# A decoder layer in split float32: the first loads in a pinned order on two DMA queues, the first casts and the first chunk in a new order

## The chip, the cores and the metric

The kernel runs on one core of a Trainium2 chip. The metric is the device time of one execution in microseconds, taken as the median over several executions. Engines are named as in the profile: PE (TensorE, matmul), PEld (its weight loads), DVE (VectorE), ACT (ScalarE), POOL (GpSimd) and SP (SyncE, which issues nearly all DMAs). A DMA is issued by an engine's instruction stream and then carried out by 16 DMA engines.

## What is computed

One decoder layer on x of 256 tokens by 1024 features, float32:

```
proj = x @ w_in                                  # 1024 -> 6 chunks of 512 columns
a = diff_attention(dq, dk, dv)                   # 4 heads, q/k pairs of 64, value 128
b = moba_attention(mq, mk, mv)                   # 8 heads of 64; at 256 tokens: causal attention
x = layer_norm(ALPHA * x + concat(a, b) @ w_o)
g, u = split(x @ w_ffn_in)                       # 2 x 2816 columns
x = layer_norm(ALPHA * x + (silu(g) * u) @ w_ffn_out)
```

Partial rotary embedding is applied to q and k.

## The kernel before

**Split products.** Every float32 operand is split into a high part, rounded to the matmul's fp32r type, and a low part, the remainder; a product is the sum of three matmuls, high·high, high·low and low·high (`mm3`, lines 141 to 144). So each weight that is loaded has to be cast by ACT (the high part) and subtracted by DVE (the low part; some pieces on POOL) before PE can use it.

**Units.** The weights are cut into units of 128 partitions x 4 rows x 512 columns, 1 MB each (line 70). Units 0 to 11 are the six chunks of w_in, two units a chunk; then w_o and the two FFN weights. `load_unit` (line 85) loads a unit in one to four DMAs on SP's queue into one of four buffers of the pool `wraw`; `split_gen` (line 98) casts on ACT (line 106) and subtracts on DVE or POOL (line 108). `ahead` (line 111 on) issues loads some units ahead, and `spread` (line 115) places the splits of the next units as hooks between the matmuls of a chunk.

**The start.** Seven matmuls on zeros (`WARM`, lines 153 and 154) run while the first data arrives. An Exp on a small tile (line 151) makes ACT load its function table. The transposed x, `xTr`, has 8 k-slices of 128 partitions x 256 tokens (128 KB each); unit 0 has four pieces `raw[0]` of 256 KB. Lines 181 to 188 issue their eight loads on SP's queue in the order w0, x0, x1, w1, x2-3, w2, w3, x4-7. Lines 189 to 194 cast and subtract them piece by piece: the cast of x0 on DVE (line 178 as `split_x` calls it), all other casts on ACT (lines 178 and 190), the subtractions on DVE (lines 179 and 192). Then `ahead` issues units 1 to 3 (line 205, three times four pieces of 256 KB), the rotary table, the causal mask, unit 4 and two small inputs.

**The chunks.** `proj_qkT` (line 384) computes the q and k chunks 0 to 3 transposed: for chunk 0 it runs over k = 0 to 7 and for each k over four column blocks j, each an `mm3` into PSUM tile j, so 96 matmuls of 256 columns. Then `rope` (line 236) takes each finished block through a shuffle, products and sums on DVE and POOL and on into high and low parts. Chunks 1 to 3, the scores, the softmax and the value chunks follow, then w_o, layer norm, the FFN (`ffn_rows`, `ffn_cols`, lines 601 and 602) and the output product (line 683), and the second layer norm with the stores at the end.

**What sets the order.** Each engine executes its own instructions strictly in the order in which they were compiled. That order is made at build time by the tile framework's scheduler, which goes by the program's order as a priority and by a simulated readiness, so instructions of one engine can pass each other. `tc.keep_in_program_order(ins)` ties an instruction behind the one traced before it on the same engine; it sets the order in the queue and adds no wait on data. From the ninth DMA on, an issue of SP waits until an earlier DMA has landed, because the framework's semaphores for these DMAs are reused.

Of the kernel before, what the change touches and what calls it, by code (L numbers as in the profile page):

```python
# [11 lines left out]
F32 = mybir.dt.float32  # L12
F32R = mybir.dt.float32r
BF16 = mybir.dt.bfloat16
AF = mybir.ActivationFunctionType
ALU = mybir.AluOpType

P = 128
S = 256
D = 1024  # L20
KT = D // P
# [3 lines left out]
HD = 64  # L25
HALF = 8
# [1 line left out]
ALPHA = 2.0 ** 0.25  # L28
LAMBDA0 = 0.8 - 0.6 * math.exp(-0.3 * 0)
EPS = 1e-5  # L30
WARM = 7


LOAD_PIECES = {1: 4, 2: 4, 3: 4, 4: 4, 5: 4, 6: 2, 7: 2}
# [22 lines left out]
def hybrid_layer_kernel(ctx, tc, xT, xr, w_in, w_o, w_f1, w_f2, cols, rows, lamb, rot, tri, out):  # L57
    nc = tc.nc
# [11 lines left out]
    units = []  # L70
# [11 lines left out]
    raw, hi, lo = {}, {}, {}  # L82
# [48 lines left out]
    def ahead(u, loads=4, splits=2):  # L131
        while state["load"] <= min(u + loads, NU - 1):
            n = state["load"]
            load_unit(n, LOAD_PIECES.get(n, 1))
            state["load"] += 1
        while state["split"] <= min(u + splits, NU - 1):
            n = state["split"]
            split_unit(n, SPLIT_PIECES.get(n, 2))
            state["split"] += 1
# [8 lines left out]
    nc.vector.memset(warm, 0.0)  # L148
    tbl = const.tile([P, 2], F32, name="tbl")
    nc.vector.memset(tbl, 0.0)  # L150
    nc.scalar.activation(tbl[:, 1:2], tbl[:, 0:1], AF.Exp)
    wps = psB.tile([P, 512], F32, tag="b", name="wps")
    for i in range(WARM):
        nc.tensor.matmul(wps, warm[:, :P], warm, start=True, stop=True)
# [5 lines left out]
    x_sb = mpool.tile([P, 2, D], F32, name="x_sb")  # L160
    axT = ctx.enter_context(ExitStack())
    xpool = axT.enter_context(tc.tile_pool(name="xpool", bufs=1))
    xTr = wraw.tile([P, KT, S], F32, tag="raw", name="xTr")
    xTh = xpool.tile([P, KT, S], F32R, name="xTh")
    xTl = xpool.tile([P, KT, S], F32R, name="xTl")
# [1 line left out]
    hi[0] = whi.tile([P, 4, 512], F32R, tag="hi", name="hi0")  # L167
    lo[0] = wlo.tile([P, 4, 512], F32R, tag="lo", name="lo0")

    def load_x(a, b):  # L170
        nc.sync.dma_start(xTr[:, a:b, :], xT[:, a:b, :])

    def load_w0(i):
        nc.sync.dma_start(raw[0][:, i, :], units[0][:, i, :])

    def split_x(a, b, copy=nc.scalar.copy):
        s = slice(a, b)
        copy(xTh[:, s, :], xTr[:, s, :])
        nc.vector.tensor_sub(xTl[:, s, :], xTr[:, s, :], xTh[:, s, :].bitcast(F32))

    load_w0(0)
    load_x(0, 1)
    load_x(1, 2)
    load_w0(1)
    load_x(2, 4)
    load_w0(2)
    load_w0(3)
    load_x(4, 8)
    for i in range(4):
        nc.scalar.copy(hi[0][:, i, :], raw[0][:, i, :])  # L190
        split_x(i, i + 1, nc.vector.tensor_copy if i == 0 else nc.scalar.copy)
        nc.vector.tensor_sub(lo[0][:, i, :], raw[0][:, i, :], hi[0][:, i, :].bitcast(F32))
    split_x(4, 6)
    split_x(6, 8)
    state["load"] = 1
    state["split"] = 1

    cs_sb = const.tile([P, 2, S], F32, name="cs_sb")
    mask = const.tile([P, S], F32, name="mask")
# [3 lines left out]
    cols_sb = const.tile([P, 1], F32, name="cols_sb")  # L203
    lam_in = const.tile([P, 4, HD], F32, name="lam_in")
    ahead(0, loads=3, splits=-1)
    for h in range(0, P, HD):
        nc.sync.dma_start(cs_sb[h : h + 2 * HALF, :, :], rot)
    nc.sync.dma_start(mask[:, P:], tri)
    ahead(0, splits=-1)
    nc.sync.dma_start(cols_sb, cols)  # L210
    nc.sync.dma_start(lam_in, bass.AP(tensor=lamb.tensor, offset=lamb.offset, ap=[[0, P], [HD, 4], [1, HD]]))
    ident = const.tile([P, P], F32, name="ident")
    make_identity(nc, ident)
    mhalf = const.tile([P, 8], F32, name="mhalf")
# [169 lines left out]
    def proj_qkT(c, side):  # L384

        pool, tag = (psB, "b") if c == 1 else (psA, "acc")
        pss = [pool.tile([P, 2, S], F32, tag=tag, name=f"pj{c}_{b}") for b in range(4 if c < 2 else 2)]
        kb = {0: 1, 1: 4}.get(c, KT)
        order = [(j, k0 + k) for k0 in range(0, KT, kb) for j in range(4) for k in range(kb)]
        fin = []  # L390
        ahead(2 * c, splits=-1)
        bg = spread([1] + [2] if c == 0 else [3, 4, 5] if c == 1 else [2 * c + 2, 2 * c + 3], 4, 28)
        for n, (j, k) in enumerate(order):
            if n == 16:
                ahead(2 * c + 1, splits=-1)
            for f in side.get(n, []) + bg.get(n, []):
                f()
            u, i = 2 * c + k // 4, k % 4
            ws = slice(j * P, (j + 1) * P)
            ps = pss[j][:, 0, :] if c < 2 else pss[j // 2][:, j % 2, :]  # L400
            mm3(ps, hi[u][:, i, ws], lo[u][:, i, ws], xTh[:, k, :], xTl[:, k, :], k == 0, k == KT - 1)
            if c == 1 and k == KT - 1:
                fin.append(rope(c, [j], ps[:, None, :]))
            if c > 1 and k == KT - 1 and j % 2:
                f = rope(c, [j - 1, j], pss[j // 2])
                if j == 1:
                    side.setdefault(n + (FIN2, FIN3)[c - 2][0], []).insert(0, f)
                else:
                    fin.append(f)
        if c == 0:  # L410
            for j in range(4):
                fin.append(rope(c, [j], pss[j][:, 0:1, :]))
        return fin
# [15 lines left out]
    fin = proj_qkT(0, {})  # L429
    nlam, gsub = lambda_prep()  # L430
    fin = proj_qkT(1, {FIN0[i]: [f] for i, f in enumerate(fin)})
    nc.sync.dma_start(x_sb, xr.rearrange("(t p) d -> p t d", p=P))
    alloc_group(0)
    sc = {FIN1[i]: [f] for i, f in enumerate(fin)}
    for j in range(4):
# [409 lines left out]
```

## Time and profile before

| | |
|---|---|
| median of 3 runs | 318.17 us (318.13 to 320.09) |
| the profiled execution | 317.75 us |
| its span, first to last instruction | 315.8 us |
| mean granted PE clock over the span | 0.991 |
| PE busy | 300.4 us, 95% of the span |
| DVE busy | 254.3 us, 81% |
| ACT busy | 177.7 us, 56% |

Times in the rows are microseconds from the span's start. Busy shares are averages over stages that have different limits, so the rows below are mostly from the first 20 us, where the change is made. "Idle before <-X" in a row of a timeline is the time for which the engine stood still just before that row and what ended it. The profiled execution is 2 us longer than its span, since launch and end lie outside the span.

### The profile page before, as it was taken

What the parts mean: (1) busy time and instruction counts of PE and PEld (TensorE: products, weight loads), DVE (VectorE), ACT (ScalarE), POOL (GpSimd) and SP (SyncE); (2) the same over time, 40 slices, a digit from 0 to 9 for tenths busy, and PEclk for the clock granted to TensorE, in tenths of its full rate; (3) what the DMA queues carried; (4) which work ended last, traced back from release to release, by engine and by line L of the source; (5) the groups of instructions that cost most, each with busy time, mean ns of one, the idle gap of its engine ahead of it and who ended that gap; (6) DMA issues with size and microseconds to landing.
All of it is one profiled execution on the core that took longest, in us unless ns stands there. A gap on an engine that the chain in (4) does not pass through costs nothing.

```text
span 315.8 us, 4704 instructions
## 1 busy us (share of the span) xinstructions
PE 300.4 (95%) x1720; PEld 255.6 (81%) x1720; DVE 254.3 (81%) x476; ACT 177.7 (56%) x347; POOL 36.3 (11%) x38
## 2 busy tenths in 40 slices
PE   8899899999999999999999999999999999999960
PEld 5799789867887788888888888888888887888850
DVE  3799999999977289949397598578679779989595
ACT  3857479398685328247377457656664565654000
POOL 1076553310030010100000000000000000000011
PEclk9999999999999999999999999999999999999996
DMA  6989943333376432558654664474362436630002
GB/s 176 391 282 352 413 151 135 133 136 137 141 251 211 195 133 66 222 247 301 230 157 146 230 221 151 162 268 162 126 246 66 175 103 227 236 127 0 0 33 100
DMA packets 13749, 57.17 MB, mean 181 GB/s; under 512 B 1664, under 2 KB 2432, under 8 KB 8864
## 3 DMA queue, kind: packets, MB, share of 16 engines
q1 hardware_dynamic: 13440, 54.79, 49.8%
q0 software_dynamic: 288, 2.10, 1.8%
q8 instruction: 13, 0.21, 0.3%
q14 instruction: 8, 0.07, 0.1%
HBM read 55.84 MB, written 1.05 MB: 180 GB/s over the span
## 4 chain that ended last, share of the span: by engine, by line
PE 74%; DVE 15%; DMA 4%; issue 3%; POOL 1%; ACT 1%; SPq 1%; DVEq 0%; ACTq 0%
PE fc L601 21%; PE foc L683 13%; PE fc L602 11%; DVE lo L108 4%; PE fo L683 4%; DMA raw<-in_w_in_dram 4%; PE wo L142 2%; PE fr L143 2%; PE fr L142 2%; PE wo L144 2%; PE wo L143 2%; PE fr L144 2%; PE pj L142 2%; PE pj L144 2%; PE pj L143 2%
## 5 line engine op out<-in xcount | busy, mean ns | idle before, releaser
L108 DVE TENSOR_TENSOR lo<-raw,hi 128x512 fp32r<-128x512 f32 (+2 forms) x108 | 105.6, 1001 | 20.9 <-ACT hi L106 20.8
L106 ACT CAST hi<-raw 128x512 fp32r<-128x512 f32 (+2 forms) x116 | 90.2, 827 | 22.5 <-PE wo L144 9.9
L601 PE MATMUL fc<-x1T,hi 128*128 128x512 f32 x288 | 100.1, 392 | 0.0
L602 PE MATMUL fc<-x1T,lo 128*128 128x256 f32 x288 | 80.5, 280 | 0.0
L601 PEld LDWEIGHTS fc<-x1T,hi 128*128 128x128 f32 x288 | 54.1, 188 | 11.9
L602 PEld LDWEIGHTS fc<-x1T,lo 128*128 128x128 f32 x288 | 54.0, 188 | 0.0
L142 PE MATMUL pj<-xTh,hi 128*128 128x256 f32 x128 | 36.7, 294 | 1.4 <-ACT hi L190 1.4
L144 PE MATMUL pj<-xTh,lo 128*128 128x256 f32 x128 | 35.7, 286 | 0.6 <-DVE lo L108 0.5
L143 PE MATMUL pj<-xTl,hi 128*128 128x256 f32 x128 | 36.1, 284 | 0.0
L604 ACT COPY v<-fc 128x256 f32<-128x256 f32 x36 | 13.3, 370 | 27.6 <-PE fc L602 27.6
L142 PEld LDWEIGHTS pj<-xTh,hi 128*128 128x128 f32 x128 | 24.3, 192 | 3.0 <-ACT hi L190 2.5
L144 PEld LDWEIGHTS pj<-xTh,lo 128*128 128x128 f32 x128 | 24.1, 191 | 1.3 <-DVE lo L108 0.7
L143 PEld LDWEIGHTS pj<-xTl,hi 128*128 128x128 f32 x128 | 24.5, 191 | 0.0
L605 DVE TENSOR_TENSOR v<-v,fc 128x256 f32<-128x256 f32 x36 | 15.0, 418 | 11.3 <-ACT v L604 11.2
L512 POOL TENSOR_TENSOR rsf<-rsf,mhalf 128x1 f32<-128x1 f32 x2 | 1.8, 922 | 178.6 <-DVE rsf L511 178.6
L683 PE MATMUL foc<-hi,hTl 128*128 128x512 f32 x56 | 22.1, 395 | 0.0
L683 PE MATMUL foc<-lo,hTh 128*128 128x512 f32 x56 | 22.1, 394 | 0.0
L683 PE MATMUL foc<-hi,hTh 128*128 128x512 f32 x56 | 22.1, 394 | 0.0
L108 POOL TENSOR_TENSOR lo<-raw,hi 128x512 fp32r<-128x512 f32 x8 | 13.8, 1723 | 20.1 <-ACT hi L106 20.1
L284 ACT ACTIVATE E<-E,negm 128x128 f32<-128x128 f32 (+1 forms) x32 | 14.2, 444 | 2.5 <-DVE negm L281 2.4
L247 POOL TENSOR_TENSOR sh<-sh,cs_sb 128x256 f32<-128x256 f32 (+1 forms) x12 | 13.3, 1120 | 18.2 <-DVE sh L245 17.5
L142 PE MATMUL pj<-hi,xTh 128*128 128x512 f32 x32 | 13.7, 429 | 0.0
(201 smaller groups left out, 547.5 us busy)
## 6 DMA issues: line engine op xcount, KB each, us to landing
raw<-in_w_f_dram SPq DMA_DIRECT2D x28, 1024.0 KB, 5.1
raw<-in_w_in_dram SPq DMA_DIRECT2D x24, 256.0 KB, 5.5
raw<-in_w_in_dram SPq DMA_DIRECT2D x4, 1024.0 KB, 6.3
raw<-in_w_o_dram SPq DMA_DIRECT2D x4, 1024.0 KB, 4.8
raw<-in_w_f_dram SPq DMA_DIRECT2D x10, 256.0 KB, 3.5
raw<-in_w_f_dram SPq DMA_DIRECT2D x5, 512.0 KB, 4.6
raw<-in_w_in_dram SPq DMA_DIRECT2D x4, 512.0 KB, 8.4
rows<-in_rows_dram POOLq DMA_DIRECT2D x2, 1024.0 KB, 6.6
```

Of the source, the lines that this page charges most:

```text
L106: nc.scalar.copy(h[:, s, :], r[:, s, :])
L108: eng.tensor_sub(l[:, s, :], r[:, s, :], h[:, s, :].bitcast(F32))
L142: nc.tensor.matmul(ps, sh, mh, start=first, stop=False)
L143: nc.tensor.matmul(ps, sh, ml, start=False, stop=False)
L144: nc.tensor.matmul(ps, sl, mh, start=False, stop=last)
L247: nc.gpsimd.tensor_mul(sh, sh, sin2[:, :m, :])
L284: nc.scalar.activation(e, e, AF.Exp, bias=negm[g][:, i, u : u + 1], scale=-1.0, accum_out=ls[g][:, i, u : u + 1])
L601: nc.tensor.matmul(ps, hi[u][:, i, ws], x1T[:, k], start=k == 0, stop=False)
L602: nc.tensor.matmul(ps[:, 0, :], lo[u][:, i, ws], x1T[:, k, 0, :], start=False, stop=k == KT - 1)
L604: nc.scalar.copy(v, ps[:, 1, :])
L605: nc.vector.tensor_add(v, v, ps[:, 0, :])
L683: nc.tensor.matmul(bank[name] if ps is None else ps, x, w[:, cs], start=key not in opened, stop=last and (m, i) == (len(todo) - 1, 2))
```

## The change

The Exp that loads ACT's table is traced behind the first x loads. x0, x1 and x2-3 are loaded on ACT's queue; w0 to w3 and then x4-7 on SP's queue, each pinned behind the load before it. The casts and subtractions of unit 0 and x are pinned in one order on ACT (w0, w1, x2-3, w2, w3, x4-5, x6-7) and one on DVE (x0 cast and both its parts, w0, x1 cast and parts, w1, x2-3, w2, w3, x4-5, x6-7): the cast of x1 moves from ACT to DVE, and x2 and x3 are cast together. Chunk 0 runs over k and, inside k, over the three products, each for all four blocks j: first high·high four times, then high weight by low x, then low weight by high x. Two more matmuls on zeros stand at the start. Five later loads (rotary table, mask, two small inputs, x itself) are pinned in the program's order.

```
-WARM = 7
+WARM = 9
...
-    nc.scalar.activation(tbl[:, 1:2], tbl[:, 0:1], AF.Exp)
...
-    load_w0(0)
-    load_x(0, 1)
-    load_x(1, 2)
-    load_w0(1)
-    load_x(2, 4)
-    load_w0(2)
-    load_w0(3)
-    load_x(4, 8)
-    for i in range(4):
-        nc.scalar.copy(hi[0][:, i, :], raw[0][:, i, :])
-        split_x(i, i + 1, nc.vector.tensor_copy if i == 0 else nc.scalar.copy)
-        nc.vector.tensor_sub(lo[0][:, i, :], raw[0][:, i, :], hi[0][:, i, :].bitcast(F32))
-    split_x(4, 6)
-    split_x(6, 8)
+    pin = tc.keep_in_program_order
+    nc.scalar.dma_start(xTr[:, 0:1, :], xT[:, 0:1, :])
+    for a, b in ((1, 2), (2, 4)):
+        pin(nc.scalar.dma_start(xTr[:, a:b, :], xT[:, a:b, :]))
+    pin(nc.scalar.activation(tbl[:, 1:2], tbl[:, 0:1], AF.Exp))
+    nc.sync.dma_start(raw[0][:, 0, :], units[0][:, 0, :])
+    for i in range(1, 4):
+        pin(nc.sync.dma_start(raw[0][:, i, :], units[0][:, i, :]))
+    pin(nc.sync.dma_start(xTr[:, 4:8, :], xT[:, 4:8, :]))
+    def first_hi(i):
+            h, l, src = hi[0][:, i, :], lo[0][:, i, :], raw[0][:, i, :]
+            pin(nc.scalar.copy(h, src))
+            return lambda: pin(nc.vector.tensor_sub(l, src, h.bitcast(F32)))
+    def first_x(a, b, eng=nc.scalar):
+        s = slice(a, b)
+        pin((eng.copy if eng is nc.scalar else eng.tensor_copy)(xTh[:, s, :], xTr[:, s, :]))
+        pin(nc.vector.tensor_sub(xTl[:, s, :], xTr[:, s, :], xTh[:, s, :].bitcast(F32)))
+    f = first_hi(0)
+    first_x(0, 1, nc.vector)
+    f()
+    first_x(1, 2, nc.vector)
+    first_hi(1)()
+    first_x(2, 4)
+    for i in (2, 3):
+        first_hi(i)()
+    first_x(4, 6)
+    first_x(6, 8)
...
+        for k in range(KT if c == 0 else 0):
+            u, i = k // 4, k % 4
+            for p, (w, x) in enumerate(((hi, xTh), (hi, xTl), (lo, xTh))):
+                if 4 * k + p == 16:
+                    ahead(1, splits=-1)
+                for f in bg.get(4 * k + p, []) + (bg.get(4 * k + 3, []) if p == 2 else []):
+                    f()
+                for j in range(4):
+                    nc.tensor.matmul(pss[j][:, 0, :], w[u][:, i, j * P : (j + 1) * P], x[:, k, :],
+                                     start=(k, p) == (0, 0), stop=(k, p) == (KT - 1, 2))
-        for n, (j, k) in enumerate(order):
+        for n, (j, k) in enumerate(order if c else ()):
```

## Rows read from the trace of the kernel before

**Rows 1.** Page, part 1: busy time of each engine over the span.
```profile
PE 300.4 (95%) x1720; PEld 255.6 (81%) x1720; DVE 254.3 (81%) x476; ACT 177.7 (56%) x347; POOL 36.3 (11%) x38
```

**Rows 2.** Chain of work that ended last, in order of time: start, length, what.
```profile
3.52 6.25 DMA raw<-in_w_in_dram
...
16.50 1.27 DVE lo L108
...
57.51 0.33 PE ppd L290
```

**Rows 3.** Busy time by stretch: engines with instruction counts, PEclk, DMA share, GB/s.
```profile
1.50:4.50 3.00, 2.96 (x8) 0.89 (x6) 0.54 (x2) 1.34 (x3) 0.42 (x3) 1.00 0.85 208
...
6.00:8.00 2.00, 2.00 (x17) 2.00 (x17) 0.69 (x1) 0.39 (x1) 0.00 (x0) 1.00 0.73 128
8.00:16.00 8.00, 6.63 (x54) 6.36 (x53) 6.36 (x11) 6.67 (x13) 0.13 (x1) 1.00 1.04 393
...
16.00:57.50 41.50, 39.64 (x323) 37.38 (x321) 40.96 (x114) 28.96 (x83) 24.24 (x18) 1.00 0.72 255
```

**Rows 4.** Timeline of SP, its DMA issues: start, length, line, what, count.
```profile
0.74 0.37 SPq L174 DMA_DIRECT2D raw<-in_w_in_dram  x1
1.17 0.89 SPq L171 DMA_DIRECT2D xTr<-in_xT_dram  x2
...
4.00 0.43 SPq L171 DMA_DIRECT2D xTr<-in_xT_dram  x1
4.47 9.66 SPq L95 DMA_DIRECT2D raw<-in_w_in_dram  x12
...
25.57 0.38 SPq L432 DMA_DIRECT2D x_sb<-in_xr_dram  x1
```

**Rows 5.** Timeline of ACT: start, length, line, what [idle before <-releaser].
```profile
0.74 1.28 ACT L151 ACT_TABLE_LOAD   x1 [0.74 <-PEq L835]
...
3.61 0.62 ACT L190 CAST hi<-raw 128x512 fp32r<-128x512 f32 x1 [1.38 <-DMA raw<-in_w_in_dram]
5.10 0.40 ACT L178 CAST xTh<-xTr 128x256 fp32r<-128x256 f32 x1 [0.87 <-DMA xTr<-in_xT_dram]
5.77 0.62 ACT L190 CAST hi<-raw 128x512 fp32r<-128x512 f32 x1 [0.27 <-DMA raw<-in_w_in_dram]
8.15 0.71 ACT L178 CAST xTh<-xTr 128x256 fp32r<-128x256 f32 x2 [1.76 <-DMA xTr<-in_xT_dram]
9.14 1.28 ACT L190 CAST hi<-raw 128x512 fp32r<-128x512 f32 x2 [0.27 <-DMA raw<-in_w_in_dram]
11.11 1.14 ACT L178 CAST xTh<-xTr 128x512 fp32r<-128x512 f32 x2 [0.69 <-DMA xTr<-in_xT_dram]
```

**Rows 6.** Timeline of PE: start, length, line, what, count [idle before <-releaser].
```profile
1.19 3.17 PE L154 MATMUL wps<-warm 128*128 128x512 bf16 x7 [1.19 <-DVE tbl L150]
4.40 1.20 PE L142 MATMUL pj<-xTh,hi 128*128 128x256 f32 x4
...
5.93 0.41 PE L143 MATMUL pj<-xTl,hi 128*128 128x256 f32 x1
6.15 0.41 PE L144 MATMUL pj<-xTh,lo 128*128 128x256 f32 x1
...
8.04 0.28 PE L143 MATMUL pj<-xTl,hi 128*128 128x256 f32 x1
8.16 0.28 PE L144 MATMUL pj<-xTh,lo 128*128 128x256 f32 x1
9.81 0.39 PE L142 MATMUL pj<-xTh,hi 128*128 128x256 f32 x1 [1.37 <-ACT hi L190]
```

**Rows 7.** Timeline of DVE: start, length, line, what [idle before <-releaser].
```profile
3.96 0.29 DVE L178 CAST xTh<-xTr 128x256 fp32r<-128x256 f32 x1 [2.81 <-DMA xTr<-in_xT_dram]
...
16.50 1.27 DVE L108 TENSOR_TENSOR lo<-raw,hi 128x512 fp32r<-128x512 f32 x1 [0.43 <-ACT hi L106]
...
17.77 0.45 DVE L245 STREAM_SHUFFLE sh<-pj 128x256 f32<-128x256 f32 x1
```

More of the change, by code (lines that the diff above doesn't have):

```diff
@@ L168, in hybrid_layer_kernel @@
     lo[0] = wlo.tile([P, 4, 512], F32R, tag="lo", name="lo0")
[L170 to L176, printed above, removed]
-        s = slice(a, b)
-        copy(xTh[:, s, :], xTr[:, s, :])
-        nc.vector.tensor_sub(xTl[:, s, :], xTr[:, s, :], xTh[:, s, :].bitcast(F32))
-    load_w0(0)
-    load_x(0, 1)
-    load_x(1, 2)
-    load_w0(1)
-    load_x(2, 4)
-    load_w0(2)
-    load_w0(3)
-    load_x(4, 8)
-    for i in range(4):
-        nc.scalar.copy(hi[0][:, i, :], raw[0][:, i, :])
-        split_x(i, i + 1, nc.vector.tensor_copy if i == 0 else nc.scalar.copy)
-        nc.vector.tensor_sub(lo[0][:, i, :], raw[0][:, i, :], hi[0][:, i, :].bitcast(F32))
-    split_x(4, 6)
-    split_x(6, 8)
+    pin = tc.keep_in_program_order
[12 more added lines that the diff above has]
+    def first_x(a, b, eng=nc.scalar):
+        s = slice(a, b)
+        pin((eng.copy if eng is nc.scalar else eng.tensor_copy)(xTh[:, s, :], xTr[:, s, :]))
[10 more added lines that the diff above has]
+    first_x(6, 8)
     state["load"] = 1
@@ L206, in hybrid_layer_kernel @@
     for h in range(0, P, HD):
-        nc.sync.dma_start(cs_sb[h : h + 2 * HALF, :, :], rot)
-    nc.sync.dma_start(mask[:, P:], tri)
+        pin(nc.sync.dma_start(cs_sb[h : h + 2 * HALF, :, :], rot))
+    pin(nc.sync.dma_start(mask[:, P:], tri))
     ahead(0, splits=-1)
-    nc.sync.dma_start(cols_sb, cols)
-    nc.sync.dma_start(lam_in, bass.AP(tensor=lamb.tensor, offset=lamb.offset, ap=[[0, P], [HD, 4], [1, HD]]))
+    pin(nc.sync.dma_start(cols_sb, cols))
+    pin(nc.sync.dma_start(lam_in, bass.AP(tensor=lamb.tensor, offset=lamb.offset, ap=[[0, P], [HD, 4], [1, HD]])))
     ident = const.tile([P, P], F32, name="ident")
@@ L431, in hybrid_layer_kernel @@
     fin = proj_qkT(1, {FIN0[i]: [f] for i, f in enumerate(fin)})
-    nc.sync.dma_start(x_sb, xr.rearrange("(t p) d -> p t d", p=P))
+    tc.keep_in_program_order(nc.sync.dma_start(x_sb, xr.rearrange("(t p) d -> p t d", p=P)))
     alloc_group(0)
```

## Prediction

> **What bounds the kernel now.** I read the busy times first, then the chain that ended last, then the first 20 us engine by engine. PE is busy for 300.4 of 315.8 us [rows 1], so it looks like the only limit; the chain corrects that. In order of time it goes through the DMAs of w_in from 3.52 us on, then from 16.50 through DVE's subtractions, and only from 57.51 us through PE [rows 2]. The busy table says the same: between 16 and 57.5 us DVE works 40.96 of 41.50 us, while PE, with 39.64, has 1.86 us of idle time [rows 3]. So a microsecond that PE gains at the start reaches the end only if DVE's work between 16 and 57.5 us is earlier too; and that work starts when weights have landed. From 8 to 16 us the DMA engines run at a share of 1.04 and 393 GB/s, which is all they give in this trace; before, they do worse: 208 GB/s from 1.5 to 4.5 us at a share of 0.85, and 128 GB/s from 6 to 8 us at a share of 0.73 [rows 3].
>
> The start in detail. SP issues the eight first loads one after another from 0.74 to 4.43 us and then the twelve pieces of units 1 to 3 from 4.47 on [rows 4]. Where a cast was released by a DMA, its start marks a landing: w0 by 3.61, x1 by 5.10, w1 by 5.77, x2-3 by 8.15, w2 by 9.14, x4-7 by 11.11 [rows 5]; x0 by 3.96 [rows 7]. PE does k = 0 and 1 from 4.40 to 8.44, idles 1.37 us for the high part of w2, and from 9.81 on runs without a gap worth naming through chunk 0 [rows 6].
>
> **The change part by part.** The sum is made against the profiled execution, 317.75 us, which lies 0.42 under the median of the three runs, 318.17; I add the 0.42 at the end. One per cent is 3.2 us, about what a measurement of this kernel can tell from no change, as its three runs lie up to 2 us apart.
>
> *Loads on two queues.* Three of SP's eight issues go to ACT: two of 0.89 together and one of about 0.43, so 1.3 us [rows 4]. SP's first piece of unit 1 could be issued at 3.1 instead of 4.47. The bytes and their sizes stay the same. Bounds: 0, if the DMA engines were never short of work, and 1.3 us, if the issue was all that held them. The nearest row is the share between 1.5 and 4.5 us, 0.85 [rows 3]: 15% of 3 us, 0.45, was not filled. I take 0.5 us: all landings behind the first four come 0.5 earlier, and with them the chain through unit 1 and DVE.
>
> The trace shows this as a bound by the DMA engines and not by SP, with shares of 0.85 and 1.04 [rows 3]. The Trainium skill says the same and more strongly, in "DMA: Bandwidth & Descriptors", section "Issuing engines are not separate DMA queues": loads started by different engines end on the same 16 DMA engines, and only the starting engine's issue time is saved. By that rule this part would be worth nearer to nothing than 1.3 us; it is the first rival below.
>
> *What ACT pays.* No DMA issue of ACT stands in the trace. By SP's rows one costs 0.37 to 0.45 us [rows 4], three cost 1.1 to 1.35. They push the table load of 1.28 us, which now starts at 0.74 [rows 5], to end at 3.1 to 3.4, and the small Exp behind it to 3.3 to 3.6; the first cast waits for w0 until 3.61 anyway [rows 5]. So 0. The cover behind it: PE is on its zero matmuls until 5.27 (next item), so the cast of 0.62 us may start as late as 4.6; beyond that each microsecond costs PE one, up to the idle 1.37.
>
> *Two more zero matmuls.* The seven run from 1.19 for 3.17 us, 0.45 each with the last one's tail shared out [rows 6], so nine end at 1.19 + 9 x 0.45 = 5.27. The first real matmul goes from 4.40 to 5.27, 0.87 later. The idle 1.37 us before 9.81 absorbs it [rows 6]: 0, with 0.5 of cover left, which is just what is used if w2 lands 0.5 earlier. In that stretch PE runs at the lower of its two levels, 1.2 GHz: 256 columns at 5.93 and 6.15 follow each other by 0.22 us, where at 8.04 and 8.16 it is 0.12 (2.4 GHz), although the table of stretches prints a granted clock of 1.00 throughout [rows 3, 6]. PE had been at work nearly without a pause from 1.19 when the spacing fell. Nine keep it at work without the pause before 4.40, so the rise should come no later. From below I bound this at 0 as well, since w2 and not PE sets 9.81.
>
> *Casts in a pinned order.* ACT loses x1's cast, 0.40 us, and DVE gains it at 0.29 [rows 5, 7]. x2 and x3 go as one cast and one subtraction instead of two. DVE has 2.81 us of idle time before its first cast [rows 7] and works 0.69 of the 2 us from 6 to 8 [rows 3]; ACT idles 1.76 before 8.15 [rows 5]. So 0. Without that cover it would be 0.29.
>
> *Product by product.* The same 96 matmuls at 0.12 us. The compiled order before already mixed the products: four high by high at 4.40, then singles of L143 and L144 [rows 6]. 0, between minus and plus 0.4, one or two more restarts of 0.2 us like the one at 9.81, whose neighbours start 0.22 and not 0.12 apart.
>
> *Later loads pinned.* In the trace SP issues x itself at 25.57, behind the tables and unit 4 [rows 4], which is the order of the program already. 0.
>
> *Downstream.* DVE's last idle time of note, 0.43 us at 16.50, waits for a cast of a landed piece, and the first shuffle of chunk 0 follows at 17.77 [rows 7]. With landings and chunk 0 both up to 0.5 earlier I take this wait as filled: 0.4. The bounds are 0 and 0.54, all that DVE idles between 16 and 57.5 [rows 3].
>
> Sum: 0.5 + 0.4 = 0.9 us. 317.75 - 0.9 = 316.85, and with 0.42 added, 317.3 us.
>
> **The rivals.**
>
> *Nothing moves (318.2).* The DMA engines, not the issue, set the landings of units 1 to 3, and DVE's stretch begins when it did. For it: the share of 1.04 at 393 GB/s from 8 to 16 us, and a share of 0.73 with 128 GB/s from 6 to 8, when eight DMAs had already been issued [rows 3, 4], so lack of issues was not the cause. Against: the share of 0.85 before 4.5.
>
> *The slow stretch goes (315.9).* From 6 to 8 us the engines moved 128 and not 393 GB/s; 265 x 2 us is 530 KB, 1.35 us at 393 GB/s [rows 3]. If it came from the single queue, the change removes it: 0.9 + 1.35 = 2.25 us. For it: the engines were not full. Against: there was work in the queue. If the 208 GB/s before 4.5 rose as well, 185 x 3 us or 555 KB, another 1.4 us, would give 314.5, the far end.
>
> *The weights come later (319.2, the slower side).* x's 512 KB on its own queue shares the DMA engines with w0 and w1 from the start. If each queue gets half, w1 is complete when 1024 KB have moved and no longer when 768 KB have; that is the place of x2-3 now, 8.15 instead of 5.77 [rows 5]. Its cast takes 0.62, and k = 1 needs 12 x 0.12 = 1.4 us: done at 10.2, 0.4 behind the 9.81 of today. PE would then idle from about 7 to 8.8, and if it runs at its lower level afterwards, 24 matmuls cost 0.1 more each, 2.4 us. So 0.4 to 2.8; DVE's wait at 16.50 hides 0.43 of it. I take 1.0. The point from which it decides: w1 later than 9.81 - 1.4 - 0.6 = 7.8 us. Against: k = 2 waits for w2 in any case, so a late w1 costs nothing until then.
>
> That the two queues take turns is what the Trainium skill states ("DMA: Bandwidth & Descriptors", section "Queues, rings and completion order": each DMA engine goes round the queues that have work, packet by packet); no run here shows it yet.
>
> **How the numbers follow.** The forecast 0.42, nothing moves 0.27, the slow stretch goes 0.16, the weights come later 0.15. The range from 315.2 to 319.0 holds the first two whole, most of the third and the milder part of the fourth. Faster by over 1% means under 315.0: the far end of the third, 0.06. Slower by over 1% means over 321.3, only the fourth with its lower level kept for long: 0.03. Within 1%: 0.91.
>
> **What would show it.** Right: on SP the first piece of unit 1 issued near 3.1 to 4.0; w2's cast before 9.0; the cast of x4-5 begun near 10.6 instead of 11.11; PE reaching its first transposes of the probabilities, the step at 57.51, about 0.9 earlier. Wrong: that step at 57.5 or later although PE's gap before k = 2 is gone (then DVE or the DMA engines held it); w1's cast after 7.8 (the slower rival); a DMA rate near 390 GB/s from 5 us on (the third). Wrong in size: a different compiled order of DVE's work after 16 us, which I could not read from the trace before.

## The result and the profile after

The changed kernel took 321.39 us in the median of nine runs (320.57 to 322.81), the kernel before 318.17 beside it (317.39 to 320.37): a ratio of 1.0096, with an interval of 1.0074 to 1.0118. So it is slower by about one per cent, where 317.3 us was forecast. The profiled execution took 320.62 us with a span of 318.5, against 317.75 and 315.8: 2.87 us more.

PE's busy time is the same within 0.2 us, so the loss is waiting. Page part 1 of the changed kernel, which answers to [rows 1]:

```profile
PE 300.2 (94%) x1722; PEld 255.7 (80%) x1722; DVE 254.5 (80%) x476; ACT 177.4 (56%) x345; POOL 35.2 (11%) x38
```

The start first. Timeline of SP in the changed kernel (columns as in [rows 4]):

```profile
0.74 0.38 SPq L175 DMA_DIRECT2D raw<-in_w_in_dram  x1
1.18 1.37 SPq L177 DMA_DIRECT2D raw<-in_w_in_dram  x3
2.59 0.52 SPq L178 DMA_DIRECT2D xTr<-in_xT_dram  x1
4.16 10.52 SPq L95 DMA_DIRECT2D raw<-in_w_in_dram  x12
```

And of ACT ([rows 5]):

```profile
0.74 0.40 ACTq L171 DMA_DIRECT2D xTr<-in_xT_dram  x1
1.17 0.94 ACTq L173 DMA_DIRECT2D xTr<-in_xT_dram  x2
2.14 1.28 ACT L174 ACT_TABLE_LOAD   x1 [2.14 <-issue]
3.44 0.20 ACT L174 ACTIVATE tbl<-tbl 128x1 f32<-128x1 f32 x1
3.98 0.62 ACT L182 CAST hi<-raw 128x512 fp32r<-128x512 f32 x1 [0.35 <-DMA raw<-in_w_in_dram]
5.06 0.62 ACT L182 CAST hi<-raw 128x512 fp32r<-128x512 f32 x1 [0.46 <-DMA raw<-in_w_in_dram]
9.81 0.62 ACT L187 CAST xTh<-xTr 128x512 fp32r<-128x512 f32 x1 [4.13 <-DMA xTr<-in_xT_dram]
10.33 1.14 ACT L182 CAST hi<-raw 128x512 fp32r<-128x512 f32 x2
11.70 1.14 ACT L187 CAST xTh<-xTr 128x512 fp32r<-128x512 f32 x2 [0.23 <-DMA xTr<-in_xT_dram]
```

Three things are to be seen. SP is through with the first loads at 3.11, yet the first piece of unit 1 goes out at 4.16 and not at 3.1. It is the ninth DMA and waits for x0, the first load of ACT's queue, as the chain of the changed kernel shows (start, length, what; x0 lands at 4.14, the first piece of unit 1 at 12.34):

```profile
0.74 3.40 DMA xTr<-in_xT_dram
...
4.16 8.18 DMA raw<-in_w_in_dram
```

w1 is cast at 5.06, earlier than 5.77. And x2-3, issued behind x1 on ACT's queue, is cast at 9.81 instead of 8.15; ACT works in the pinned order, so w2 and w3 stand behind it and are cast from 10.33 on instead of 9.14.

The trace records the landing of each load. w0 and x0 land at 3.96 and 4.14, w1 and x1 at 5.04 and 5.22, w2 and x2-3 at 9.62 and 9.78: the loads of the two queues arrive in pairs, one of each, although w0 and w1 carry twice the bytes of x0 and x1. The kernel before had x2-3 at 8.13 and w2 at 9.11. So x2-3 lost its lead: it was 0.98 ahead of w2 and is now 0.17 behind. In all five profiles with x2-3 on ACT's queue it is 0.17 to 0.20 behind. As its cast stands ahead of w2's, w2 is cast 0.71 after it has landed, where before it was 0.03.

w2 itself landed 0.51 later as well, and for this the bytes have to be counted. Here are the DMA queues from 6 to 8 us (queue, packets, MB, share of the 16 engines; q1 carries SP's loads, q10 ACT's):

```profile
q1 hardware_dynamic: 149, 0.34, 58.2%
q10 hardware_dynamic: 58, 0.10, 39.1%
```

ACT's queue moved less than a quarter of the bytes, for it had only x2-3 left to carry, and eight of the sixteen shares into which a load is cut had landed by 7.40; SP's queue went on with later loads. The table of stretches ([rows 3]) says how much was moved in all:

```profile
1.50:4.50 3.00, 3.00 (x8) 1.06 (x7) 0.30 (x2) 2.00 (x3) 0.42 (x3) 1.00 0.80 256
4.50:6.00 1.50, 1.50 (x7) 1.28 (x6) 1.47 (x4) 0.72 (x2) 0.00 (x0) 1.00 0.72 202
6.00:8.00 2.00, 2.00 (x15) 2.00 (x14) 0.79 (x2) 0.00 (x0) 0.00 (x0) 1.00 0.97 218
8.00:16.00 8.00, 5.98 (x51) 5.77 (x50) 5.54 (x10) 5.89 (x11) 0.00 (x0) 1.00 0.99 357
```

The second of these stretches in the kernel before:

```profile
4.50:6.00 1.50, 1.50 (x7) 1.46 (x8) 1.21 (x3) 0.63 (x2) 0.00 (x0) 1.00 0.99 357
```

More came through than before in the first and the third stretch (256 against 208 GB/s, 218 against 128), less in the second and the fourth (202 against 357, 357 against 393). Up to 8 us that makes 1.51 MB against 1.42, up to 16 us 4.36 against 4.56. The 0.2 MB that are missing take 0.5 us at 393 GB/s, and by about as much w2 and the loads behind it are late. That is no more than two executions of one kernel differ by: w2 landed at 9.95 in a second profile of the kernel before (below). PE pays first at k = 2 ([rows 6]):

```profile
1.19 4.02 PE L153 MATMUL wps<-warm 128*128 128x512 bf16 x9 [1.19 <-DVE tbl L150]
4.66 1.42 PE L407 MATMUL pj<-xTh,hi 128*128 128x256 f32 x4
...
11.00 0.75 PE L407 MATMUL pj<-xTh,hi 128*128 128x256 f32 x4 [2.02 <-ACT hi L182]
```

That is 1.19 us later than 9.81, but it isn't the end of the story: the first score matmul comes only 0.75 later (38.78 against 38.03), and then the loss grows, to 1.88 at the first transpose of the probabilities (59.00 against 57.12) and to 2.4 at the score matmuls of the next chunk (72.28 against 69.88). From about 84 us on it stays at 2.65. The first transposes before and after:

```profile
57.12 0.33 PE L289 MATMUL ppd<-ident,E 128*128 128x128 f32 x1 [0.62 <-DVE E L306]
```

```profile
59.00 0.33 PE L294 MATMUL ppd<-ident,E 128*128 128x128 f32 x1 [1.78 <-DVE E L311]
```

So some three quarters of a microsecond come from the start and two from between 43 and 74 us, where the change edits nothing. PE's waits in the changed kernel (what waited, for whom, us in total, times, longest):

```profile
PE pj L407 <- ACT hi L182: 2.0, 1, 2.0
PE ppd L294 <- DVE E L311: 1.8, 1, 1.8
PE wps L153 <- DVE tbl L150: 1.2, 1, 1.2
PE s L142 <- DVE negm L286: 1.1, 1, 1.1
```

In the kernel before, the wait of ppd is 0.6 us, and the one for negm is not in the list. Both are waits for DVE, so here is DVE's timeline between 49 and 59 us. Before:

```profile
49.60 0.74 DVE L245 STREAM_SHUFFLE sh<-pj 128x512 f32<-128x512 f32 x1
50.24 0.67 DVE L246 TENSOR_TENSOR a<-pj,cs_sb 128x512 f32<-128x512 f32 x1
50.83 1.49 DVE L108 TENSOR_TENSOR lo<-raw,hi 128x512 fp32r<-128x512 f32 x1
52.25 0.68 DVE L251 TENSOR_TENSOR a<-a,sh 128x512 f32<-128x512 f32 x1
52.85 0.24 DVE L301 RECIPROCAL rl<-ls 128x16 f32<-128x16 f32 x1
...
55.70 3.74 DVE L306 SCALAR_TENSOR_TENSOR E<-E,sc 128x128 f32<-128x128 f32 x8
```

After:

```profile
49.49 0.69 DVE L108 TENSOR_TENSOR lo<-raw,hi 128x512 fp32r<-128x512 f32 x1 [0.17 <-ACT hi L106]
...
51.22 0.74 DVE L250 STREAM_SHUFFLE sh<-pj 128x512 f32<-128x512 f32 x1
51.85 0.68 DVE L251 TENSOR_TENSOR a<-pj,cs_sb 128x512 f32<-128x512 f32 x1
52.63 0.25 DVE L306 RECIPROCAL rl<-ls 128x16 f32<-128x16 f32 x1
53.43 1.76 DVE L256 TENSOR_TENSOR a<-a,sh 128x512 f32<-128x512 f32 x1 [0.55 <-POOL sh L252]
55.11 1.28 DVE L108 TENSOR_TENSOR lo<-raw,hi 128x512 fp32r<-128x512 f32 x2
...
56.73 0.68 DVE L108 TENSOR_TENSOR lo<-raw,hi 128x512 fp32r<-128x512 f32 x1
57.33 1.23 DVE L308 TENSOR_SCALAR sc<-sc,nlam 128x8 f32<-128x8 f32 x1
58.60 2.72 DVE L311 SCALAR_TENSOR_TENSOR E<-E,sc 128x128 f32<-128x128 f32 x8
```

The same instructions stand in another order. Before, the weight split at 50.83 runs while POOL makes its part of sh, and the add behind it finds sh ready. After, that split has been taken forward to 49.49, where it waits 0.17 us for its cast, pushes the shuffle back by its own 0.6 and leaves the add to wait 0.55 for POOL. One more split (56.73) stands ahead of the scaling of E, where before it came behind. E begins 2.90 us later than before, though the score matmuls ahead of it began only 0.75 late.

The lengths of these rows say something too. The same split takes 0.68 us at 54.02 and 1.49 at 50.83, the first scaling of E 0.34 in the changed kernel and 1.36 before, the add at 53.43 takes 1.76 instead of 0.68. Each of the long ones stands beside an instruction of POOL. POOL's timeline of the kernel before:

```profile
50.49 1.28 POOL L247 TENSOR_TENSOR sh<-sh,cs_sb 128x512 f32<-128x512 f32 x1 [6.41 <-DVE sh L245]
...
55.39 1.52 POOL L108 TENSOR_TENSOR lo<-raw,hi 128x512 fp32r<-128x512 f32 x1 [1.31 <-ACT hi L106]
```

The split at 50.83 ends at 52.32, 0.55 behind POOL's 51.77, and the first scaling of E at 57.06, behind POOL's 56.91; the add at 53.43 ends at 55.19, and POOL is at work on a split of its own from 53.36 to 54.64. So these instructions of DVE got little done while POOL worked. It is not so for all: the mask products from 42.84 to 44.02 kept their usual 0.28 and 0.42 us beside POOL's work from 42.80 to 44.08. By such rows some 6 of the 40.96 us for which DVE is busy from 16 to 57.5 us are waiting beside POOL (an estimate: what an instruction lasted beyond the length it has when POOL is idle). The long first scaling is also why PE's loss at 59.00 is 1.88 and not the 2.90 of E's start. No run tried POOL's part by itself.

The order on each engine is set when the program is compiled; in the changed kernel's compiled list DVE's instructions stand otherwise in eleven places behind 43 us, and ACT's in five. The experiments separate the loads from that order.

### The profile page after: what moved, and what is told of

Same layout as the page of the kernel before. It is cut to its first block, busy times and chain, and to the rows that moved or that the text cites. A ratio compares the mean times of both kernels' runs of the same rounds, so it can differ in the third digit from the quotient of the medians.

```text
span 318.5 us, 4704 instructions
## 1 busy us (share of the span) xinstructions
PE 300.2 (94%) x1722; PEld 255.7 (80%) x1722; DVE 254.5 (80%) x476; ACT 177.4 (56%) x345; POOL 35.2 (11%) x38
## 4 chain that ended last, share of the span: by engine, by line
PE 72%; DVE 14%; DMA 5%; issue 3%; ACT 2%; POOL 2%; DVEq 0%; ACTq 0%; POOLq 0%; SPq 0%
PE fc L617 21%; PE foc L699 13%; PE fc L618 11%; DMA raw<-in_w_in_dram 4%; PE fo L699 4%; DVE lo L108 3%; PE wo L142 2%; PE fr L143 2%; PE fr L142 2%; PE wo L143 2%; PE wo L144 2%; PE fr L144 2%; PE pj L142 2%; DVE a L256 2%; PE pj L144 2%
## 5 line engine op out<-in xcount | busy, mean ns | idle before, releaser
L142 PE MATMUL pj<-xTh,hi 128*128 128x256 f32 x96 | 27.8, 289 | 0.0
L144 PE MATMUL pj<-xTh,lo 128*128 128x256 f32 x96 | 27.1, 282 | 0.4 <-DVE lo L108 0.4
L143 PE MATMUL pj<-xTl,hi 128*128 128x256 f32 x96 | 27.0, 281 | 0.0
L144 PEld LDWEIGHTS pj<-xTh,lo 128*128 128x128 f32 x96 | 18.1, 188 | 0.6 <-DVE lo L108 0.6
L142 PEld LDWEIGHTS pj<-xTh,hi 128*128 128x128 f32 x96 | 18.1, 188 | 0.5
L143 PEld LDWEIGHTS pj<-xTl,hi 128*128 128x128 f32 x96 | 18.1, 188 | 0.0
L108 POOL TENSOR_TENSOR lo<-raw,hi 128x512 fp32r<-128x512 f32 x8 | 12.8, 1606 | 20.7 <-ACT hi L106 20.7
```

What stands on the lines that cost most here:

```text
L108: eng.tensor_sub(l[:, s, :], r[:, s, :], h[:, s, :].bitcast(F32))
L142: nc.tensor.matmul(ps, sh, mh, start=first, stop=False)
L143: nc.tensor.matmul(ps, sh, ml, start=False, stop=False)
L144: nc.tensor.matmul(ps, sl, mh, start=False, stop=last)
```

## The experiments

An order can be tied without changing a wait: a table gives the instruction numbers of each engine, and each is made to follow the one before it on its own engine. The edit, common to all runs that tie an order (called ORDER below; PE's order is the same in all of them but for added zero matmuls):

```diff
+ORDER = {
+    "DVE": [
...
+    have = {i.name: i for i in nc.cur_bb.bb.instructions}
+    for chain in ORDER.values():
+        chain = [n for n in chain if f"I-{n}" in have]
+        for a, b in zip(chain, chain[1:]):
+            tc.add_manual_dep(have[f"I-{b}"], f"I-{a}",
...
```

All diffs are against the changed kernel; where a line is a list of numbers, the minus line is that kernel's compiled order and the plus line the order that the run ties, in the numbers of the changed kernel. The kernel before, run beside the experiments, had medians of 318.06, 318.18 and 318.04 us in three sets of 25, 31 and 35 runs.

**One queue, the rest kept.** The eight loads go back to SP in their old order.

```diff
-    nc.scalar.dma_start(xTr[:, 0:1, :], xT[:, 0:1, :])
-    for a, b in ((1, 2), (2, 4)):
-        pin(nc.scalar.dma_start(xTr[:, a:b, :], xT[:, a:b, :]))
...
+    pin(nc.sync.dma_start(xTr[:, 0:1, :], xT[:, 0:1, :]))
+    pin(nc.sync.dma_start(xTr[:, 1:2, :], xT[:, 1:2, :]))
+    pin(nc.sync.dma_start(raw[0][:, 1, :], units[0][:, 1, :]))
+    pin(nc.sync.dma_start(xTr[:, 2:4, :], xT[:, 2:4, :]))
...
```

> The changed kernel with its eight first loads back on SP's queue in the old order (w0, x0, x1, w1, x2-3, w2, w3, x4-7), all else as changed: nine zero matmuls, pinned casts, chunk 0 product by product. In the compiled program the orders of DVE, ACT and POOL behind unit 0 are then those of the kernel before. Theory A (x2-3 lands late on the second queue, 9.81 us instead of 8.15, and all behind it): x2-3's cast again near 8.2, PE resumes near 9.8, time about 318.2. Theory B (the compiled order of DVE, ACT and POOL after 16 us costs): also about 318.2, since that order is undone as well. Theory C (pinned casts or nine zero matmuls cost): stays near 320.5 to 321.4.

Measured: 318.38 us, ratio 1.0017 (0.9986 to 1.0048). Behind the first unit this kernel's DVE, ACT and POOL have the order of the kernel before, but for one split and one shuffle that change places near 18 us. So the zero matmuls, the pinned casts, the product order and the later pins cost nothing that can be measured; the loss hangs on the two queues and on what follows from them.

**Two queues in the old order.** The changed kernel tied to the order of the run above.

```diff
-349, 312, 315, 323, 326,
+312, 315, 323, 326, 349,
...
-756, 727, 729, 731, 733, 746, 747,
+727, 729, 731, 733, 746, 747, 756,
...
```

These are the first changed stretch of DVE's list and the first of its late part, by instruction number: 756 is the split seen at 49.49, 746 and 747 are the shuffle and the product behind it.

> The changed kernel with its loads on two queues, but every instruction of PE, DVE, ACT and POOL tied behind its predecessor in the compiled order of the one-queue kernel (which, behind unit 0, is the order of the kernel before on DVE, ACT and POOL). Theory A (late landings alone): the loss stays whole, about 321. Theory B (compiled order alone): about 318.2. Both: PE resumes at k = 2 near 11.0 and chunk 0 ends near 19.6, but the wait at the first transposes of the probabilities shrinks from 1.8 us; time between, about 319.5 to 320.

Measured: 320.78 us, 1.0056 (1.0025 to 1.0088), in two groups of times: 318.8 to 319.9 in four of ten executions, 320.8 to 321.6 in six. x2-3 is cast at 10.19 and PE idles 2.6 us ahead of k = 2; the wait of ppd is back at 0.6. The median is that of the theory that the late landing is all (about 321), but the profile isn't: with the first group the two queues by themselves cost some 0.5 us against the run above, and the second group had to be explained.

**One queue in the new order.** The converse: loads as in the first run, tied to the changed kernel's order.

```diff
-        pin(nc.scalar.dma_start(xTr[:, a:b, :], xT[:, a:b, :]))
+    pin(nc.sync.dma_start(xTr[:, 2:4, :], xT[:, 2:4, :]))
...
+ORDER = {
...
```

> The opposite mix: loads on one queue in the old order, every instruction of PE, DVE, ACT and POOL tied into the compiled order of the changed kernel. Theory A: about 318.2. Theory B: about 321, with the wait of 1.8 us at the first transposes still there. Both: about 319.5 to 320.

Measured: 320.35 us, 1.0057 (1.0033 to 1.0081), with the waits of the changed kernel: 1.8 us for E and 1.0 for negm. The order costs some 2 us with no load moved. The theory that the late landing is all (318.2) misses.

**The kernel before, once more.** No edit; a single execution.

> The kernel before, unchanged, for a second profile of its start: if the slow stretches of the DMA engines (128 GB/s from 6 to 8 us in the first profile) come by chance, they lie elsewhere here and x2-3's and w2's casts move by more than 0.5 us from 8.15 and 9.14; if they belong to the order of the loads, the casts start within 0.3 us of those.

Measured: 318.57 us. The casts of x2-3, w2 and x4-5 came 0.8 us later than in [rows 5] (8.93, 9.97, 11.95), the rate from 6 to 8 us was again low (100 GB/s), and the end was 0.82 later. Neither alternative holds: the casts moved by more than 0.5 us, but the slow stretch of the DMA engines stood in the same place. Its length differed between these two executions by about as much as the forecast meant to gain, and by as much as the changed kernel's first score matmul was late: it came at 38.88 here, against 38.03 and 38.78.

**Only the late part of the new order.** One queue; DVE from its 61st instruction and ACT from its 36th in the changed kernel's order, all ahead of that in the old one. The loads are edited as above; of the order:

```diff
-349, 312, 315, 323, 326,
+312, 315, 323, 326, 349,
...
```

> Loads on one queue; PE, POOL and the first 60 DVE instructions in the order of the kernel before, but DVE from its 61st and ACT from its 36th instruction on (the scores of the first head group and later) in the compiled order of the changed kernel. There, one subtraction of unit 8 stands before the last scores and no longer behind the second shuffle of chunk 2, where it ran while POOL multiplied. If that late part is the price of the order: about 320.2 as with the whole new order on one queue, with a wait near 1.8 us at the first transposes of the probabilities. If the early part (splits of units 3 to 5 against the rotary sums) is the price: about 318.4, with a wait near 0.6.

Measured: 320.75 us, 1.008 (1.0049 to 1.0112), again with 1.8 us for E and 1.1 for negm. The late part is the price of the order.

**Only x0 and x1 on ACT's queue**, the rest of x on SP behind w1, in the old order:

```diff
-    for a, b in ((1, 2), (2, 4)):
-        pin(nc.scalar.dma_start(xTr[:, a:b, :], xT[:, a:b, :]))
+    pin(nc.scalar.dma_start(xTr[:, 1:2, :], xT[:, 1:2, :]))
...
+    pin(nc.sync.dma_start(xTr[:, 2:4, :], xT[:, 2:4, :]))
```

> Only x0 and x1 (256 KB) on ACT's queue; x2-3 back on SP's queue behind w1; compiled order of the kernel before everywhere behind the loads. If the price of the two queues is x2-3's place on a queue of its own beside SP's long one: x2-3's cast starts by 8.9 and the time is 318.2 to 318.6, or up to 0.9 less since SP issues two loads fewer. If any second queue at the start slows the landings: w2's cast behind 10, time 319.5 or more.

Measured: 318.28 us, 0.9987 (0.9957 to 1.0017). x2-3 is cast at 7.13, a microsecond earlier than in [rows 5], but w2 still at 9.18, and PE idles 1.4 us ahead of k = 2. Both are as the first alternative had it: the price was x2-3's place. Taking two issues off SP is worth nothing that can be measured.

**x2-3 late, on one queue**: w2 and w3 are issued ahead of it, old order.

```diff
+    pin(nc.sync.dma_start(raw[0][:, 2, :], units[0][:, 2, :]))
+    pin(nc.sync.dma_start(raw[0][:, 3, :], units[0][:, 3, :]))
+    pin(nc.sync.dma_start(xTr[:, 2:4, :], xT[:, 2:4, :]))
```

> One queue, compiled order of the kernel before, but w2 and w3 are issued before x2-3. The slow stretch of the DMA engines (100 to 210 GB/s from 6 to 8 us in every one-queue profile): if it belongs to the time after the start, it stands there again; if it belongs to x2-3's transfer, it moves behind 7. ACT casts x2-3 before w2, so PE resumes when x2-3 has landed, as late as w3 did (about 10); time 318.5 to 319.5, which also says what 0.5 us of later start for k = 2 costs when the loads behind are not later.

Measured: 320.05 us, 1.0048 (1.002 to 1.0076), in two groups again: 318.4 to 319.4 in five executions, 320.7 to 321.8 in five. The median misses the 318.5 to 319.5 expected; the first group is about there. The slow stretch stands again from 6 to 8 us, with 180 GB/s. The profiled execution is of the second group. Its table of stretches:

```profile
8.00:10.00 2.00, 0.39 (x4) 0.18 (x2) 0.00 (x0) 0.61 (x2) 0.00 (x0) 1.00 1.03 339
10.00:12.00 2.00, 1.42 (x7) 1.42 (x8) 1.96 (x4) 2.00 (x6) 0.00 (x0) 0.72 0.98 350
12.00:14.00 2.00, 2.00 (x12) 2.00 (x11) 2.00 (x4) 1.97 (x5) 0.00 (x0) 0.50 1.06 406
```

The seventh number is the granted clock. PE works 0.39 of the 2 us before 10; then the clock is at half, the lower level of 1.2 GHz, from about 11 us to the end of these rows. PE's timeline of the same run shows the pause of 2.19 us ahead of it and groups of four matmuls that start 0.80 apart and, next, 0.85: 0.21 for one, where 0.12 is usual here:

```profile
10.58 1.00 PE L555 MATMUL pj<-xTh,hi 128*128 128x256 f32 x4 [2.19 <-ACT hi L330]
11.38 1.05 PE L555 MATMUL pj<-xTl,hi 128*128 128x256 f32 x4
```

**Two queues, late part old.** The changed kernel with its own order up to 43 us and the old one behind (the complement of the run with the late part alone):

```diff
-756, 727, 729, 731, 733, 746, 747,
+727, 729, 731, 733, 746, 747, 756,
...
```

> The changed kernel on two queues with its own early order, but DVE from its 61st and ACT from its 36th instruction on in the order of the kernel before. If the late part of the order is worth about 1.8 us: 319.5 to 320, with the wait at the first transposes back near 0.6; if only the early part counts, 321.

Measured: 318.50 us, 1.0000 (0.9976 to 1.0023), although x2-3 is cast at 9.42 and PE idles 2.5 us ahead of k = 2. That is less than the 319.5 to 320 expected. With the late order undone and the early one kept, the change costs nothing that can be measured. It doesn't follow that two queues are free: in the wholly old order they cost some 0.5 us, above, and what the early part of the new order gives back was not tried apart.

**One late stretch of two.** DVE's 89th to 111th instruction, and ACT's casts beside them, put back:

```diff
-756, 727, 729, 731, 733, 746, 747, 804, 771, 785, 796, 773, 805, 824, 806,
+727, 729, 731, 733, 746, 747, 756, 771, 804, 805, 785, 773, 806, 796, 807,
```

Here 824 is the split at 56.73, 771 the add, 804 the reciprocal, and 807 and those behind it the scaling of E.

> The changed kernel with one stretch of its compiled order put back: VectorE's 89th to 111th instruction (mask products, the split lo8, the reciprocal, the first sums) and ScalarE's two casts beside them stand as in the kernel before; the later stretch (sums against splits behind the probabilities) stays the changed kernel's. Theory (this stretch is the larger part of the loss): the wait ahead of the first ppd matmul falls from 1.8 to 0.6 to 0.8 us, the negm wait further on stays near 1 us, and the median comes to 320.0 to 320.5 (ratio 1.005 to 1.007) against 321.4 of the changed kernel. Rival 1 (the whole loss is here): 318.3 to 319.2. Rival 2 (it is the later stretch): the ppd wait may fall but the median stays at 321 or more.

Measured: 319.81 us, 1.0064 (1.0037 to 1.009). PE's waits:

```profile
PE s L289 <- DVE negm L433: 1.4, 1, 1.4
...
PE ppd L441 <- DVE E L458: 0.6, 1, 0.6
```

The wait for E is mended, the one for negm is longer by 0.3. The ratio lies in the range of the theory, the median a little under its 320.0 to 320.5; both rivals miss. That this stretch is the larger part of the loss is not borne out: the table at the end of this section has the changed kernel lose 1.91 us behind the first score matmul, and this one 1.37.

**Zero matmuls in PE's idle stretch**, on two queues in the old order:

```diff
+                for _ in range(8 if (k, p) == (2, 0) else 0):
+                    nc.tensor.matmul(wps, warm[:, :P], warm, start=True, stop=True)
                 for j in range(4):
```

> Two queues in the old compiled order (as in e2_two_queues_old_order), plus eight zero matmuls on TensorE between the products of the second weight tile and those of the third, where it sat idle 2.6 us. Eight at 0.22 us fill about 1.8 us of that. Theory (the upper group of times, 320.8 to 321.5 in 6 of 10 executions, is a granted clock that falls after the idle stretch): the clock stays at its upper level from 8 to 16 us, the upper group is gone, and the median comes to 318.8 to 319.2. Rival (the upper group has another cause, the loads or the order): six of ten executions still read 320.8 or more and the median stays above 320.

Measured: 319.01 us (318.09 to 319.46 in twelve executions), 1.0019 (1.0000 to 1.0037). The upper group of the same kernel without them, six of ten at 320.8 or more, is gone, as the theory of the clock had it.

**The same eight on one queue** in the old order: the loads of the first run, and the lines just shown.

```diff
-        pin(nc.scalar.dma_start(xTr[:, a:b, :], xT[:, a:b, :]))
+    pin(nc.sync.dma_start(xTr[:, 2:4, :], xT[:, 2:4, :]))
...
+                for _ in range(8 if (k, p) == (2, 0) else 0):
...
```

> One queue in the old order (as in e1_one_queue, which is the kernel before but for the pins, the zero matmuls and the product order), plus the same eight zero matmuls in the idle stretch ahead of the third weight tile, 1.2 us in that profile. Theory (clock): no execution at 320 or more where e1 had three of ten; the fillers overrun the idle stretch by up to 0.6 us, so the median stands at 318.2 to 318.8. Rival: two to four of ten executions still read 320 or more; or the overrun costs more, median 319 or above.

Measured: 318.37 us (318.11 to 318.80), 1.0009 (0.9993 to 1.0024). Table of stretches:

```profile
8.00:10.00 2.00, 2.00 (x13) 1.13 (x12) 0.89 (x3) 1.24 (x2) 0.00 (x0) 1.00 0.97 340
10.00:12.00 2.00, 2.00 (x18) 1.97 (x18) 1.40 (x4) 1.37 (x3) 0.00 (x0) 1.00 1.04 380
```

PE never stops, its clock stays at the upper level, and no execution is above 319, where the first run had three of ten at 320.3 to 320.9. The median stays: what the upper times lost is saved, the others pay nothing. The run before differs from this one by the queues alone, so with PE kept at work the two queues cost 0.64 us in the old order (319.01 against 318.37).

**The best parts together**: x0 and x1 alone on ACT's queue, the changed kernel's order up to 43 us, the old one behind, and the eight zero matmuls.

```diff
+    pin(nc.sync.dma_start(xTr[:, 2:4, :], xT[:, 2:4, :]))
...
-756, 727, 729, 731, 733, 746, 747,
+727, 729, 731, 733, 746, 747, 756,
...
+                for _ in range(8 if (k, p) == (2, 0) else 0):
...
```

> The parts that measured well put together: first two tiles of x on ScalarE's queue and the rest on SyncE's (as in e6_x01_on_act), the changed kernel's compiled order up to 43 us and the old one behind it (as in e8_two_queues_late_old), and eight zero matmuls in the idle stretch. Theory: it beats both kernels slightly, 317.2 to 317.9 (ratio 0.996 to 0.999), with no execution above 319. Rival (the gains don't add, or the fillers delay the third tile's products): 318.2 to 318.8, no difference from the kernel before.

Measured: 318.07 us (317.44 to 318.89), 0.9996 (0.998 to 1.0012). It doesn't beat the kernel before in the median: it lies between the 317.2 to 317.9 of the theory and the 318.2 to 318.8 of the rival, and no difference from the kernel before is what the rival said. That no execution is above 319 is what the theory said. What it removes is the upper times: the kernel before had seven of 35 between 319.6 and 320.1 in the same set, all with a mean granted clock of 0.984 or 0.985, and this one has none of twelve.

**What the profiles of all runs say of the late part.** In each profile the time from the first score matmul to the end of the span was taken (us; the start of the first score matmul in the second column):

| | first score matmul | from there to the end |
|---|---|---|
| kernel before | 38.03 | 277.80 |
| kernel before, once more | 38.88 | 277.78 |
| one queue, the rest kept | 38.42 | 277.81 |
| two queues in the old order | 39.63 | 277.81 |
| two queues, late part old | 39.13 | 277.86 |
| changed kernel | 38.78 | 279.71 |
| one queue in the new order | 38.52 | 279.69 |
| one late stretch of two put back | 37.92 | 279.17 |

All ten profiles with the late part in the old order have 277.78 to 277.86, whatever the queues and the start; the new one adds 1.9 us. (The run with the late part alone has 281.12; its profiled execution, 323.94 us, was its slowest, and the granted clock fell in it once more, near 77 us.) Of the 1.9, 1.13 are lost up to the first transposes, by the order around 50 us, and 0.78 behind them; with the stretch around 50 us put back, 1.37 are lost behind them, so the two do not simply add.

## Why the prediction was wrong

*Right.* ACT's three issues cost what was said (1.34 us against 1.1 to 1.35), the table load and the small Exp ended at 3.42 and 3.64, a little beyond what was said, and the first cast waited for w0 all the same. The two zero matmuls, the casts, the product order and the later pins were put at nothing; all four together measured 1.0017 (0.9986 to 1.0048). One reason was wrong beside a right term: the spacing of PE's matmuls fell from 0.21 to 0.12 us at 7.15 and not at 6.4 as before, so the two more zero matmuls did not keep the rise from coming later; the pause ahead of k = 2 covered it. That SP's issue was not what held the loads was the rival "nothing moves", and the run with x0 and x1 alone on ACT's queue bears it out.

*The step "Loads on two queues" failed in its sign.* It had all landings 0.5 us earlier and unit 1 issued from 3.1 on. Unit 1 was issued from 4.16 on, for the ninth DMA waits for an earlier landing, as the section on the kernel before says; the step left that wait out. w1 was cast 0.71 earlier. Unit 1's first piece landed at 12.34 and not 11.75, which is within what executions of one kernel differ by (12.60 in the second profile of the kernel before), so there the moved issue shows neither gain nor loss. x2-3 was cast 1.66 later and with it w2, by 1.19. The mistake was to speak of landings as one: on one queue x2-3 was issued ahead of w2, in the order of need; on two it arrived with w2. The step bounded the gain from below at 0, and 0.64 us were lost where it could be measured cleanly (319.01 against 318.37).

The rival "the weights come later" saw the danger on the wrong side. It shared the bytes by halves, which made w1 late; w1 was earlier and x2-3 late. The Trainium skill's rule that the DMA engines go round the queues packet by packet ("DMA: Bandwidth & Descriptors", section "Queues, rings and completion order") fits the pairs: 3.96 and 4.14, 5.04 and 5.22, 9.62 and 9.78 us. Each of these six loads has 128 rows, of 2 KB in w0, w1, w2 and x2-3 and of 1 KB in x0 and x1, so turns that are counted in rows and not in bytes bring x0 in with w0, x1 with w1 and x2-3 with w2. By that count x2-3 beside w2 could have been foreseen.

*The step "Downstream" failed in its premise*, and that is where the time went. It took DVE's work after 16 us to be the same list in the same order, to be shifted as a whole, and priced the shift at 0.4. The list was compiled anew. None of the three signs of being wrong came; the last sentence of the prediction named the order as unread and gave it neither a price nor a chance, and the slower side was filled with a load mechanism alone. It could have been bounded from rows: DVE works 40.96 of 41.50 us there [rows 3], so a split of 0.68 us that is taken ahead of what PE waits for could reach the end almost whole. Three such moves would be 2 us (an estimate, and the three are hindsight); on top of the 318.2 of "nothing moves" that is 320.2, a slower rival that the text lacked. The bound of 0.54 us, all that DVE idles, took DVE's busy time for its own work; part of it is waiting beside POOL.

What the runs show in its place of the 0.4 us gain: the new late order costs 1.9 us behind the first score matmul in the profiles (279.7 against 277.8), and 2.0 to 2.4 on one queue in the medians (320.35 and 320.75 against 318.38); put back to the old one on two queues, with the early order kept, the loss is gone (1.0000). It falls apart into a stretch around 50 us and one around 65 us. The 0.75 us by which the first score matmul was late is another matter: it goes on to the end whole, but the kernel before differs by as much from itself (38.03 and 38.88), so this pair of profiles cannot put it down to the queues. The parts do not account for the 3.2 us between the medians to better than half a microsecond: 1.9 for the order, up to 0.6 for the queues, and a rest that goes with the clock, as five of the nine executions of the changed kernel are at 321.4 to 322.8 with a mean granted clock of 0.979 to 0.985, and four at 320.6 to 321.1 with 0.986 to 0.988. What in the program makes the compiler choose the one order or the other was not tried.

## What to carry to other kernels

Where a scheduler sets each engine's order, a change at the start is two changes, the one that is written and the reordering of all that follows; compare the compiled lists, or tie the order, before reading a gain or a loss into the edit. Put on a second queue only what is needed at another time than the first queue's loads: here the loads of one queue arrived in the order of issue, and those of two in pairs, so x2-3 lost the second by which it had been ahead of w2. When an engine is full, as DVE was here, any work that can wait must stand behind the work that another engine waits for. The time beside POOL's work is no free place for it, as the split at 50.83 shows: it took 1.49 us there and 0.68 elsewhere.

## What the runs showed of the hardware

The times of this kernel fall into two groups, and the clock of TensorE tells them apart: in the kernel before 317.4 to 318.5 us at a mean granted clock of 0.986 to 0.991, and 319.6 to 320.1 at 0.984 or 0.985 (28 and 7 of 35 runs). In four profiled executions of the experiments the clock stood at the lower level for some 3 us between 10 and 16 us, each time after PE had idled ahead of k = 2, for 1.86, 2.33, 2.19 and 2.47 us. The pause alone doesn't decide it: the changed kernel's profile has one of 2.02 us without a fall, two others 2.17 and 2.58. Eight zero matmuls in the pause took the upper group away in all 36 executions of three kernels. What decides in a single execution stays open.

The rate from 6 to 8 us was low in all seven profiles on one queue, 100 to 222 GB/s against 330 and more in the two microseconds behind, also where the loads stood in another order (180 GB/s with x2-3 late). It is tied to the time and not to one load; its cause was not tried. With loads on both queues it was 213 to 276 GB/s in seven profiles, and w2 landed no earlier for it where x2-3 was on ACT's queue: at 8.73 to 9.98 us, against 8.64 to 9.95 in the six profiles with x2-3 ahead of it on SP's. In this stretch the sixteen shares of a load drift apart: those of w0 landed within 0.75 us of each other in the kernel before, those of w2 from 6.29 to 9.11, and a cast waits for the last.
